# Recurrence's local part in pairs of tiles, its elementwise work on VectorE; the triangular solve and the queries in other places

## Chip, cores and metric

One core of a Trainium2 chip runs the whole program. The time is device microseconds (us) of one execution; of several executions the median is taken. Engines: TensorE (PE, its weight loads PEld), VectorE (DVE), ScalarE (ACT), GpSimd (POOL), SyncE (SP, which here issues most DMAs, in order).

## What is computed

A block of two layers (neighbourhood attention, grouped-query attention, each with a gated side branch) and then a third layer, which the change is about: a norm, eight heads of sparse attention (compressed, selected and window branches, mixed by gates), eight heads of an RWKV-7 recurrence, an output projection with a residual, and a final norm. S is 512 tokens, the width 1024, a head 64 wide. The recurrence, cut to what matters:

```
p = p + shift_mu * (prev - p)                  # prev: the token before
r, k, v, wd, ad = split(p)
decay = exp(-exp(-softplus(-(w0 + tanh(wd) @ w_up)) - 0.5));  a = sigmoid(a0 + ad @ a_up)
kk = normalise(k * k_k);  k = k * (1 + (a - 1) * k_a)
for each token t:   sa = state @ -kk_t
                    state = state * w_t + outer(sa, kk_t * a_t) + outer(v_t, k_t);  y_t = state @ r_t
y = group_norm(y) * gn_w + gn_b + sum(r * k * r_k) * v;   out = x + concat(o_nsa, y * silu(g)) @ w_out
```

## The kernel before

Tokens lie on partitions in four tiles of 128 (TT = 4). A float32 operand of a product is split into a high and a low part: `fetch` casts a weight unit on ScalarE (L147, `whi`) and subtracts on VectorE or GpSimd (L148, `wlo`); `N.lo` says which. The heads of the recurrence go in two halves `hh` of four heads (256 columns). The first two layers hold the tokens in a permuted order; `natural` (L322) copies the activations into the order of time, 16 copies, 8 on VectorE and 8 on ScalarE.

The third layer's part around the change runs so. (1) The last stage of the second layer ends in `middle_norm`, whose rows L710 (`hn`) feed the transposes of all later products. (2) `rwkv_proj_first` (L804) computes r, k and v of half 0, stages them in two activation tiles and stores rows of 768 columns in DRAM (`d_raw`, L812; a second copy holds the shifted mixture). (3) `rwkv_lowrank` (L747) makes decay and `a` of all tokens: one projection, a tanh, eight products `sc` (L769), eight tanh L771 into a ring of two tiles, each stored by ScalarE's queue (`d_low`, L774). (4) r of half 1, then in the next block `rwkv_consts` (L724, which also clears a tile, L733, and writes it over `d_t` in eight DMAs, L736), k and v of half 1, and `natural`. (5) `rwkv_local` (L827), eight times (half, tile): it loads `low` (L837) and the two copies of r, k, v (L841, four buffers `rkv` for both), adds them (L844), normalises k with a Newton rsqrt on 4 columns (L236 to L249), forms cumulated decays on TensorE (`xa`, L865), the transposed factors (L890), the 64-column products `x` (L920), masks them in two instructions per head (L925, L926), applies them to v (L928, L930), and stores six kinds of rows. Six elementwise operations of a tile are GpSimd's: L847, L848, L939, L940, L944, L945. (6) `rwkv_triangles` (L948) loads all 8 x 16 blocks of 32 x 32 (`d_a`, L951); `rwkv_solve` (L957) inverts them with 54 pairs of a multiply (L967) and a subtract (L969) on VectorE, and stores `d_t` (L972). (7) Per tile `rwkv_applied` loads `d_t` (L995) and applies it (L1003) to give K and U (L1015); `rwkv_chain` then walks the state through two chunks of 64 tokens (`VU`, L1042); `rwkv_out` makes the output rows (stored L1105). (8) `nsa_group` (L1297) is the attention of two groups of four heads, 32 blocks of two heads each with a softmax row `n_P` (L1352, L1355, L1359); (9) the output projection (L216, first add L1400) and the final norm end the program.

What sets the order: the program is written in the order above, but between (5) and (8) the generator `products()` (L1581) interleaves the attention's keys, the recurrence's gates (`rwkv_gates`), the queries (`nsa_rows`: L1229 transposes, L1233 `n_qr`) and the scores, and `tail(n)` advances the generator of (7), `steps`, or the outputs, `outs`, at the product numbers of the table `at` (L1599); the numbers from 100 on count blocks of `nsa_group`. Within that a scheduler that simulates a timeline fixes the order of instructions on each engine, and each engine runs its own in order.

```
                next(steps if nxt[1] else outs, None)
                nxt = next(at, None)
```

## Time and profile before

| | |
|---|---|
| median of 3 runs | 1234.04 us (1232.77 to 1237.34) |
| the profiled execution | 1231.49 us, of it the span 1229.7 us |
| busy in the span: PE, PEld, DVE | 1141.6, 1001.5, 847.8 us |
| ACT, POOL | 623.7, 401.8 us |
| instructions | 20522 |
| mean granted TensorE clock | 0.969 of full speed |

The profiled execution is 2.55 us below the median, and 1.8 us of it lie outside the span. Times in the trace count from the start of the span. Busy time of PE holds modelled ends of pipelined matmuls, so that 93% is not 93% of what the engine could do.

### The profile page before, as it was taken

To read this page: it belongs to the slowest core of one execution; us is meant where nothing else is said; L and a number is where in the kernel's file an instruction comes from. 1 tells how busy PE (TensorE), PEld (TensorE's weight loads), DVE (VectorE), ACT (ScalarE), POOL (GpSimd) and SP (SyncE) were. 2 spreads that over 40 slices of the span, in tenths; PEclk is the share of its full clock that TensorE was granted. 3 is DMA by queue.
4 is the path that set the end of the run, shared out by engine and by line. 5 is a ranking of instruction groups with operands and counts; after the bars stand their busy time and mean duration, and the time that the engine had idled before them with its cause. 6 is when DMAs were issued, how large, how long until landed. Compare 5 with 4: busy or idle time off the path is not lost.

```text
span 1229.7 us, 20522 instructions
## 1 busy us (share of the span) xinstructions
PE 1141.6 (93%) x7176; PEld 1001.5 (81%) x7176; DVE 847.8 (69%) x2097; ACT 623.7 (51%) x1355; POOL 401.8 (33%) x553
## 2 busy tenths in 40 slices
...
GB/s 247 116 104 103 104 98 95 99 53 141 88 102 90 82 35 1 69 38 32 52 146 66 149 107 205 239 225 180 192 167 175 162 137 103 241 45 78 189 35 69
DMA packets 87041, 143.26 MB, mean 116 GB/s; under 512 B 21525, under 2 KB 52245, under 8 KB 86938
## 3 DMA queue, kind: packets, MB, share of 16 engines
...
HBM read 114.12 MB, written 27.79 MB: 115 GB/s over the span
## 4 chain that ended last, share of the span: by engine, by line
PE 61%; DVE 18%; DMA 6%; ACT 6%; issue 5%; POOL 3%; SPq 2%; ACTq 0%; DVEq 0%; POOLq 0%
PE mm L205 24%; PE mm L188 5%; PE mm L189 5%; PE mm L190 5%; PE sc L205 3%; PE mm L216 2%; PE u L677 1%; PE tr L492 1%; DVE KT L967 1%; PE tr L670 1%; DVE big L969 1%; PE ch L1003 1%; PE tr L318 1%; DMA rkv<-d_raw 1%; PE u L205 1%
## 5 line engine op out<-in xcount | busy, mean ns | idle before, releaser
L205 PE MATMUL mm<-whi,act 128*128 128x256 f32 (+2 forms) x1344 | 357.4, 324 | 8.7 <-DVE x L347 3.3
L205 PE MATMUL mm<-wlo,act 128*128 128x256 f32 (+2 forms) x896 | 287.5, 321 | 0.4 <-POOL wlo L148 0.4
L205 PEld LDWEIGHTS mm<-whi,act 128*128 128x128 f32 x1344 | 240.9, 195 | 30.2 <-DVE x L347 5.6
L205 PEld LDWEIGHTS mm<-wlo,act 128*128 128x128 f32 x896 | 174.9, 195 | 10.3 <-POOL wlo L148 0.6
L147 ACT CAST whi<-wraw 128x1024 fp32r<-128x1024 f32 (+1 forms) x128 | 133.3, 1043 | 91.5 <-PE mm L205 36.8
L205 PE MATMUL mm<-whi,half 128*128 128x256 f32 (+1 forms) x448 | 145.6, 326 | 3.6 <-DVE half L222 3.6
L148 DVE TENSOR_TENSOR wlo<-wraw,whi 128x1024 fp32r<-128x1024 f32 x87 | 109.7, 1263 | 52.0 <-ACT whi L147 50.0
L148 POOL TENSOR_TENSOR wlo<-wraw,whi 128x1024 fp32r<-128x1024 f32 (+2 forms) x41 | 99.6, 2434 | 132.0 <-DVE rs_y L237 69.9
L188 PE MATMUL mm<-act,whi 128*128 128x512 f32 x312 | 125.4, 402 | 2.7 <-DVE b_qn L547 2.7
L190 PE MATMUL mm<-act,wlo 128*128 128x512 f32 x312 | 124.4, 399 | 0.0
L205 PEld LDWEIGHTS mm<-whi,half 128*128 128x128 f32 x448 | 87.8, 196 | 10.2 <-DVE half L222 4.5
L484 POOL TENSOR_SCALAR a_P<-a_P,a_rd 128x256 f32<-128x256 f32 x64 | 32.9, 517 | 156.6 <-DVE a_rd L483 143.9
L189 PE MATMUL mm<-half,whi 128*128 128x512 f32 x200 | 79.1, 396 | 0.0
L188 PEld LDWEIGHTS mm<-act,whi 128*128 128x128 f32 x312 | 59.6, 191 | 14.4 <-issue 3.6
L190 PEld LDWEIGHTS mm<-act,wlo 128*128 128x128 f32 x312 | 59.5, 191 | 12.0
L663 POOL TENSOR_SCALAR b_P<-b_P,b_rd 128x512 f32<-128x512 f32 x64 | 45.5, 715 | 54.8 <-DVE b_rd L662 44.2
L660 ACT ACTIVATE b_P<-sc,b_mn 128x512 f32<-128x512 f32 x64 | 44.1, 690 | 21.5 <-DVE b_mn L657 13.5
L657 DVE TENSOR_REDUCE b_mn<-sc 128x1 f32<-128x512 f32 x64 | 43.5, 684 | 10.9 <-PE sc L655 10.4
L478 DVE CUSTOM_DVE_ANT_0 a_P<-sc,a_bias 128x256 f32<-128x256 f32 x64 | 26.1, 422 | 34.7 <-PE tr L492 20.1
L222 DVE TENSOR_TENSOR b_pl<-tr,b_ph 128x512 fp32r<-128x512 f32 x64 | 43.3, 683 | 6.0 <-ACT b_ph L221 5.3
L1359 POOL TENSOR_SCALAR n_P<-n_P,b_rd,n_gl 128x128 f32<-128x128 f32 (+3 forms) x64 | 39.0, 616 | 25.5 <-DVE b_rd L1357 6.4
L189 PE MATMUL mm<-act,whi 128*128 128x512 f32 x112 | 45.3, 404 | 0.0
...
## 6 DMA issues: line engine op xcount, KB each, us to landing
...
```

The costliest lines, as they stand in the source:

```text
L147: nc.scalar.copy(hi[:, :m], raw[:, :m])
L148: self.lo.tensor_tensor(lo[:, :m], raw[:, :m], hi[:, :m].bitcast(F32), op=OP.subtract)
L188: nc.tensor.matmul(ps, lhsT=wh[:, kt], rhs=ah[:, kt], start=kt == 0, stop=False)
L189: nc.tensor.matmul(ps, lhsT=wh[:, kt], rhs=al[:, kt], start=False, stop=False)
L190: nc.tensor.matmul(ps, lhsT=wl[:, kt], rhs=ah[:, kt], start=False, stop=kt == KT - 1)
L205: nc.tensor.matmul(ps, lhsT=l, rhs=r, start=i == 0, stop=i == len(ops) - 1)
L222: (eng_lo or nc.vector.tensor_sub)(lo, src, hi.bitcast(F32))
L484: nc.gpsimd.tensor_scalar(w, w, rd, 0.5, op0=OP.mult, op1=OP.mult)
L657: nc.vector.tensor_reduce(mn, ps, axis=AX.X, op=OP.max, negate=True)
L660: nc.scalar.activation(pt, ps, AF.Exp, bias=mn, scale=1.0, accum_out=den)
L663: nc.gpsimd.tensor_scalar(pt, pt, rd, 0.5, op0=OP.mult, op1=OP.mult)
L1359: nc.gpsimd.tensor_scalar(w, w, rd, st["gl"][:, b, gc:gc + 1], op0=OP.mult, op1=OP.mult)
```

## The change

- The eight DMAs that clear `d_t` go into the first layer, from a tile that GpSimd clears.
- r, k and v of half 0 are staged in a ring of four tiles (`pp`) and stored group by group in rows of 256 columns; the two activation tiles are not used for it.
- `natural` stands right behind the projection of half 0; the low-rank part and half 1 use the natural order. The rows of half 1 are then contiguous in DRAM.
- The low-rank part's shift is one VectorE operation instead of three, its ring has three tiles, and its constants are loaded ahead of its projection.
- The local part takes two tiles at a time: inputs of both, one rsqrt on 8 columns, then each tile. The six GpSimd operations of a tile go to VectorE; the scaling of `kr` goes from VectorE (L856) to four ScalarE instructions; the two masks of a head become one of 512 columns. `raw` and `x` get rings of their own (two and three). `d_a` and `d_aq` are stored per pair of heads.
- The solve is a generator: four of its 31 steps after each of the products 8 to 15. The queries (`nsa_rows`) stand ahead of the gates, and the table `at` has other numbers.

```diff
--- before.py
+++ after.py
@@ -724,16 +724,19 @@
     def rwkv_consts(self, pool):
         nc = self.nc
         for name, shape, n in (("tri", [P, 3, P], 384), ("ind", [P, 2], 2)):
-            raw = pool.tile([P, 768], F32, name="rkv", bufs=4)[:, :n]
+            raw = pool.tile([P, 768], F32, name="rkv", bufs=3)[:, :n]
             nc.sync.dma_start(out=raw, in_=self.a[name].rearrange("p a n -> p (a n)") if n > 2 else self.a[name])
             r = pool.tile(shape, F32R, name=name, bufs=1)
             nc.vector.tensor_copy(r.rearrange("p a n -> p (a n)") if n > 2 else r, raw)
             setattr(self, name + "_r", r)
-        zero = pool.tile([P, 768], F32, name="rkv", bufs=4)
-        nc.vector.memset(zero, 0.0)
+
+    def zero_inverses(self, pool):
+        nc = self.nc
+        zero = pool.tile([P, 512], F32, name="zero", bufs=1)
+        nc.gpsimd.memset(zero, 0.0)
         for t in range(TT):
             for h in range(2):
-                nc.sync.dma_start(out=self.head_rows(self.d_t, t, 4 * h, 4), in_=zero[:, :512].rearrange("p (h n) -> p h n", h=4))
+                nc.sync.dma_start(out=self.head_rows(self.d_t, t, 4 * h, 4), in_=zero.rearrange("p (h n) -> p h n", h=4))
...
+        ps = self.cols(("r_wa",), act)
+        d = buf[:, 0]
+        nc.scalar.mul(d, ps, rest)
+        nc.vector.scalar_tensor_tensor(d[:, 1:], ps[:, :S - 1], mu, d[:, 1:], op0=OP.mult, op1=OP.add)
...
-                nc.tensor.matmul(ps, lhsT=l[0:65, t * P:t * P + P], rhs=m[0:65], start=True, stop=True)
-                th = buf[:, 6 + t % 2]
+                nc.tensor.matmul(ps, lhsT=l[:, t * P:t * P + P], rhs=m, start=True, stop=True)
+                th = buf[:, (1, 6, 7)[(4 * j + t) % 3]]
...
-                for t in range(2 * hh):
+                for t in range(2):
                     for d, a in zip(self.d_raw[hh], r):
-                        o = bass.AP(tensor=d.tensor, offset=d.offset + (1 + 16 * (2 * tp + t)) * 768 + 256 * n, ap=[[768, 16], [64 * 768, 8], [1, 256]])
+                        o = (1 + (16, P)[hh] * (2 * tp + t)) * 768 + 256 * n
+                        o = bass.AP(tensor=d.tensor, offset=d.offset + o, ap=[[[768, 16], [64 * 768, 8]], [[768, P]]][hh] + [[1, 256]])
                         nc.sync.dma_start(out=o, in_=a[:, t])
-
-    def rwkv_proj_first(self, act, mu):
-
-        raw = [self.act_tile(self.act, j, F32).rearrange("p k n -> p (k n)") for j in range(2)]
-        full = [a[:, :TT * 768].rearrange("p (t n) -> p t n", t=TT) for a in raw]
-        self.rwkv_proj(act, 0, "rkv", mu, lambda n, tp: [a[:, 2 * tp:2 * tp + 2, 256 * n:256 * n + 256] for a in full])
-        for t in range(TT):
-            for d, a in zip(self.d_raw[0], full):
-                o = bass.AP(tensor=d.tensor, offset=d.offset + (1 + 16 * t) * 768, ap=[[768, 16], [64 * 768, 8], [1, 768]])
-                self.nc.sync.dma_start(out=o, in_=a[:, t])
-        return [a[:, TT * 768:].rearrange("p (a t n) -> p a t n", a=2, t=2) for a in raw]
...
-    def rwkv_local(self, pool, hh, t, par, st):
+    def rwkv_inputs(self, pool, hh, t, par, ss):
 
         nc = self.nc
         tmp = lambda: pool.tile([P, 256], F32, name="rt", bufs=13)
         heads = lambda ap: ap.rearrange("p (h d) -> p h d", d=HD)
         V = nc.vector
-        G = nc.gpsimd
         cs = slice(256 * hh, 256 * hh + 256)
-
         low = pool.tile([P, 2, 256], F32, name="low", bufs=2)
         nc.sync.dma_start(out=low, in_=self.d_low[:, t, :, cs].rearrange("j p n -> p j n"))
-        raw = pool.tile([P, 3, 256], F32, name="rkv", bufs=4)
-        x = pool.tile([P, 3, 256], F32, name="rkv", bufs=4)
+        raw = pool.tile([P, 3, 256], F32, name="rkv0", bufs=2)
+        x = pool.tile([P, 3, 256], F32, name="rkv", bufs=3)
         for o, dst, d in zip((1, 0), (raw, x), self.d_raw[hh]):
             nc.sync.dma_start(out=dst.rearrange("p n m -> p (n m)"), in_=d[o + P * t:o + P * t + P])
-        L, a1 = low[:, 0], low[:, 1]
+        a1 = low[:, 1]
         km, kr = tmp(), tmp()
         V.tensor_tensor(x, x, raw, op=OP.add)
         r, k, v = (x[:, n] for n in range(3))
         nc.sync.dma_start(out=self.d_v[t, :, cs], in_=v)
-        G.tensor_tensor(kr, k, par["k_k"], op=OP.mult)
-        G.tensor_tensor(km, a1, par["k_a"], op=OP.mult)
+        V.tensor_tensor(kr, k, par["k_k"], op=OP.mult)
+        V.tensor_tensor(km, a1, par["k_a"], op=OP.mult)
         V.scalar_tensor_tensor(k, km, 1.0, k, op0=OP.add, op1=OP.mult)
         sq = km
         nc.scalar.activation(sq, kr, AF.Square)
+        V.tensor_reduce(ss, heads(sq), axis=AX.X, op=OP.add)
+        return low, x, kr
+
+    def rwkv_local(self, pool, hh, tp, par, st):
+
         ss = self.small.tile([P, 8], F32, name="l_ss")
-        V.tensor_reduce(ss[:, :4], heads(sq), axis=AX.X, op=OP.add)
-        V.tensor_scalar(ss[:, :4], ss[:, :4], 1e-24, None, op0=OP.max)
-        rs = self.rsqrt(ss[:, :4], 4, "l")
-        V.tensor_tensor(heads(kr), heads(kr), rs[:, :4, None].to_broadcast([P, 4, HD]), op=OP.mult)
+        parts = [self.rwkv_inputs(pool, hh, 2 * tp + j, par, ss[:, 4 * j:4 * j + 4]) for j in range(2)]
+        self.nc.vector.tensor_scalar(ss, ss, 1e-24, None, op0=OP.max)
+        rs = self.rsqrt(ss, 8, "l")
+        for j in range(2):
+            self.rwkv_tile(pool, hh, 2 * tp + j, par, st, parts[j], rs[:, 4 * j:4 * j + 4])
+
+    def rwkv_tile(self, pool, hh, t, par, st, part, rs):
+        nc = self.nc
+        tmp = lambda: pool.tile([P, 256], F32, name="rt", bufs=13)
+        heads = lambda ap: ap.rearrange("p (h d) -> p h d", d=HD)
+        V = nc.vector
+        cs = slice(256 * hh, 256 * hh + 256)
+        low, x, kr = part
+        L, a1 = low[:, 0], low[:, 1]
+        r, k, v = (x[:, n] for n in range(3))
+        for h in range(4):
+            w = slice(64 * h, 64 * h + 64)
+            nc.scalar.mul(kr[:, w], kr[:, w], rs[:, h:h + 1])
         V.scalar_tensor_tensor(a1, a1, 1.0, kr, op0=OP.add, op1=OP.mult)
...
-        ab = pool.tile([P, 4, 2, P], F32, name="abq", bufs=2)
...
+            ab = pool.tile([P, 2, 2, 2, P], F32, name="abq", bufs=2)
...
-                am = pool.tile([P, 256], F32, name="am", bufs=2)
-                V.tensor_tensor(am, ps[:, 0:256], mask, op=OP.mult)
-                V.tensor_tensor(ab[:, h].rearrange("p a n -> p (a n)"), ps[:, 256:512], mask, op=OP.mult)
+                V.tensor_tensor(ab[:, e].rearrange("p j a n -> p j (a n)"), ps.rearrange("p (j n) -> p j n", j=2),
+                                mask[:, None, :].to_broadcast([P, 2, 256]), op=OP.mult)
+                am = ab[:, e, 0].rearrange("p a n -> p (a n)")
...
-        nc.sync.dma_start(out=self.head_rows(self.d_a, t, 4 * hh, 4), in_=ab[:, :, 0])
-        for c in range(2):
-            w = slice(64 * c, 64 * c + 64)
-            nc.sync.dma_start(out=self.d_aq[t, w, 4 * hh:4 * hh + 4], in_=ab[w, :, 1, w])
+            h = 4 * hh + 2 * pr
+            nc.sync.dma_start(out=self.head_rows(self.d_a, t, h, 2), in_=ab[:, :, 1, 0])
+            for c in range(2):
+                w = slice(64 * c, 64 * c + 64)
+                nc.sync.dma_start(out=self.d_aq[t, w, h:h + 2], in_=ab[w, :, 1, 1, w])
         nc.sync.dma_start(out=self.d_y0[t, :, cs], in_=y0.rearrange("p r n -> p (r n)"))
         kg = tmp()
-        G.tensor_tensor(kg, k, e2, op=OP.mult)
-        G.tensor_tensor(e2, b, e2, op=OP.mult)
+        V.tensor_tensor(kg, k, e2, op=OP.mult)
+        V.tensor_tensor(e2, b, e2, op=OP.mult)
         for j, src in enumerate((e2, kg)):
             nc.sync.dma_start(out=self.d_kb[t, j, :, cs], in_=src)
         sq = tmp()
-        G.tensor_tensor(sq, r, k, op=OP.mult)
-        G.tensor_tensor(sq, sq, par["r_k"], op=OP.mult)
+        V.tensor_tensor(sq, r, k, op=OP.mult)
+        V.tensor_tensor(sq, sq, par["r_k"], op=OP.mult)
...
                                         op=OP.mult)
                 nc.vector.tensor_tensor(tv, tv, o, op=OP.subtract)
+            yield
...
+                        if (hf, t) == (1, 0):
+                            N.zero_inverses(pool)
...
-                    rest = N.rwkv_proj_first(act, N.rwkv_mu(pool, 0, 0, 3, "mu0"))
+                    ring = lambda n, tp: [pool.tile([P, 512], F32, name="pp", bufs=4).rearrange("p (t n) -> p t n", t=2) for _ in range(2)]
+                    N.rwkv_proj(act, 0, "rkv", N.rwkv_mu(pool, 0, 0, 3, "mu0"), ring)
+                    act = N.natural(act)
                     N.rwkv_lowrank(pool.tile([P, 8, S], F32, name="low", bufs=1), act)
-                    N.rwkv_proj(act, 1, "r", N.rwkv_mu(pool, 1, 0, 1, "mu1"), lambda n, tp: [a[:, tp] for a in rest])
+                    N.rwkv_proj(act, 1, "r", N.rwkv_mu(pool, 1, 0, 1, "mu1"), ring)
...
-                act = N.natural(act)
...
-                    for t in range(TT):
-                        N.rwkv_local(loc, hh, t, par, st)
+                    for tp in range(2):
+                        N.rwkv_local(loc, hh, tp, par, st)
...
-            N.rwkv_solve(chn, *sv)
+            solve = N.rwkv_solve(chn, *sv)
...
+                for _ in N.nsa_rows(keep, pool, act, st, ns):
+                    yield
                 for _ in N.rwkv_gates(pool, act):
-                    yield
-                for _ in N.nsa_rows(keep, pool, act, st, ns):
                     yield
...
-            at = iter(((10, 1), (14, 1), (14, 0), (14, 1), (21, 0), (21, 1), (100, 0), (100, 1), (102, 0)))
+            at = iter(((17, 1), (18, 1), (18, 0), (19, 1), (20, 0), (20, 1), (100, 0), (100, 1), (102, 0)))
...
             for n, _ in enumerate(products()):
+                for _ in range(4 if 8 <= n < 16 else 0):
+                    next(solve, None)
                 tail(n)
```

**SyncE, ahead of the first tile's loads.** `d_t` are the inverses, `low` and `d_raw` the inputs of the local part, `wraw` weights. Before:

```order
78 L728 DMA rkv<-in_ind 128x2
79 L780 DMA mu<-in_shift_mu 128x2x256
80 L686 DMA k_k<-in_k_k 128x256
81 L736 DMA d_t<-rkv 128x4x128 x8
82 L686 DMA k_a<-in_k_a 128x256
83 L686 DMA r_k<-in_r_k 128x256
84 L837 DMA low<-d_low 128x2x256
85 L802 DMA d_raw_84<-st_8768 16x8x256 x2
86 L802 DMA d_raw_83<-st_8767 16x8x256 x2
87 L841 DMA rkv<-d_raw_81 128x768
```

After:

```order
91 L728 DMA rkv<-in_ind 128x2
92 L789 DMA mu<-in_shift_mu 128x2x256
93 L686 DMA k_k<-in_k_k 128x256
94 L686 DMA k_a<-in_k_a 128x256
95 L686 DMA r_k<-in_r_k 128x256
96 L834 DMA low<-d_low 128x2x256
97 L838 DMA rkv_9028<-d_raw_81 128x768
98 L812 DMA d_raw_84<-st_8820 128x256 x2
99 L838 DMA rkv<-d_raw_82 128x768
```

The eight clears are gone from this place, and the first `rkv` load stands right behind the first `low` load.

**VectorE, the solve.** `big` are the blocks and their inverses, `n_qr` and `st` belong to queries and gates; a wait in brackets names the engine or DMA queue waited for. Before, its start:

```order
1453 L967 TENSOR_TENSOR KT<-big_10239,big_10237 128x31 [waits DMAHW3_49,DVE_49]
1454 L407 SCALAR_TENSOR_TENSOR st_11057<-st_11057,mm 128x512 [waits Activation_49]
1455 L969 TENSOR_TENSOR big_10239<-big_10239,KT 128x31 [waits DVE_49]
1456 L967 TENSOR_TENSOR KT<-big_10239,big_10237 128x60 [waits DMAHW7_49,DVE_49]
1457 L969 TENSOR_TENSOR big_10239<-big_10239,KT 128x2x30 [waits DVE_49]
```

After, a part of its middle:

```order
1484 L984 TENSOR_TENSOR KT<-big_10201,big_10199 128x112 [waits DVE_49]
1485 L407 SCALAR_TENSOR_TENSOR st_11384<-st_11384,mm 128x512 [waits Activation_49]
1486 L984 TENSOR_TENSOR KT<-big_10201,big_10199 128x140 [waits DVE_49]
1487 L986 TENSOR_TENSOR big_10201<-big_10201,KT 128x8x14 [waits DVE_49]
1488 L1251 TENSOR_TENSOR n_qr<-mm,n_qr 64x512 [waits DMAHW7_49,Activation_49]
1489 L986 TENSOR_TENSOR big_10201<-big_10201,KT 128x10x14 [waits DVE_49]
1490 L984 TENSOR_TENSOR KT<-big_10201,big_10199 128x104 [waits DVE_49]
```

Before, seven instructions of gates and queries stand among the solve's 108 (rows 1453 to 1565); after, 19 of queries, scores and gates do (rows 1425 to 1546).

**VectorE, ahead of the first softmax row.** `VU`, `K`, `U` and `state` are the recurrence, `n_pc` the scores, `n_P` the softmax row. Before:

```order
1638 L1015 TENSOR_TENSOR K<-ch,z 128x256 [waits PE_49,Activation_49]
1639 L1015 TENSOR_TENSOR U<-ch,z 128x256
1640 L222 TENSOR_TENSOR n_pcl<-tr,n_pch 128x512 [waits DMAHW1_49,Activation_49]
1641 L1329 COPY n_Vp<-n_Vc 32x128 [waits Pool_49]
1642 L1329 COPY n_Vp<-n_Vc 32x128 x3
1643 L1352 ISA n_P,b_mn<-sc,causal 128x128 [waits DMAHW6_49]
```

After:

```order
1566 L1060 TENSOR_TENSOR VU<-cs,U 64x512 [waits PE_49]
1567 L1347 COPY n_Vp<-n_Vc 32x128 x3
1568 L222 TENSOR_TENSOR n_pcl<-tr,n_pch 128x512 [waits DMAHW2_49,Activation_49]
1569 L1071 TENSOR_TENSOR state_10226<-cs,state_10226 64x4x64 [waits DVE_49,PE_49]
1570 L1071 TENSOR_TENSOR state_10226<-cs,state_10226 64x4x64 [waits DVE_49]
1571 L1064 TENSOR_TENSOR state_10227<-state_10226,GC 64x4x64 [waits DVE_49] x2
1572 L1033 TENSOR_TENSOR K<-ch,z 128x256 [waits PE_49,Activation_49]
1573 L1033 TENSOR_TENSOR U<-ch,z 128x256
1574 L1370 ISA n_P,b_mn<-sc,causal 128x128 [waits DMAHW1_49]
```

Before, 78 rows stand between the solve's last subtract and the first softmax row, four `VU` among them; after, 28, with two `VU`: the second `VU` is the end of the first tile's chain.

## Rows read from the trace of the kernel before

**Rows 1.** Stretches: us; PE, PEld, DVE, ACT, POOL busy (count); clock; DMA share; GB/s

```profile
695.00:711.00 16.00, 13.11 (x84) 11.16 (x83) 15.38 (x50) 11.20 (x20) 0.00 (x0) 1.00 0.57 178
767.00:798.00 31.00, 21.80 (x147) 21.07 (x146) 10.93 (x19) 13.29 (x15) 7.01 (x9) 0.84 0.77 240
798.00:935.00 137.00, 125.69 (x917) 115.82 (x917) 114.20 (x285) 60.30 (x189) 65.72 (x76) 0.87 0.60 186
947.00:985.50 38.50, 29.53 (x212) 27.34 (x211) 37.66 (x115) 8.49 (x12) 20.06 (x22) 0.92 0.60 181
985.50:1071.60 86.10, 78.34 (x590) 71.12 (x588) 38.92 (x83) 24.29 (x40) 25.61 (x39) 0.94 0.54 161
1071.60:1157.60 86.00, 82.11 (x646) 73.41 (x646) 75.94 (x284) 63.35 (x173) 58.54 (x78) 1.00 0.31 105
1157.60:1229.70 72.10, 58.22 (x299) 47.19 (x297) 40.36 (x106) 27.78 (x61) 31.17 (x28) 0.94 0.18 64
```

**Rows 2.** Timeline of ScalarE ahead of the first tile: start, us, instruction, idle before

```profile
771.13 7.63 ACT L330 CAST act<-half 128x512 fp32r<-128x512 f32 x7
778.67 0.58 ACT L771 ACTIVATE low<-sc 128x512 f32<-128x512 f32 x1
...
792.65 0.40 ACT L221 CAST rt_lh<-low 128x256 fp32r<-128x256 f32 x1 [9.77 <-DMA low<-d_low]
```

**Rows 3.** Timeline of SyncE's queue there

```profile
780.54 6.34 SPq L736 DMA_DIRECT2D d_t<-rkv  x8
...
788.65 0.43 SPq L837 DMA_DIRECT2D low<-d_low  x1
```

**Rows 4.** Timelines there, TensorE's first `xa` and VectorE's first add

```profile
793.11 0.58 PE L865 MATMUL xa<-rt_lh,tri 128*128 128x256 f32 x1 [6.81 <-ACT rt_lh L221]
...
798.07 0.96 DVE L844 TENSOR_TENSOR rkv<-rkv 128x768 f32<-128x768 f32 x1 [3.81 <-DMA rkv<-d_raw]
```

**Rows 5.** Waits from 765 to 940: us in total, times, longest

```profile
ACT rt_lh L221 <- DMA low<-d_low: 26.3, 7, 9.8
...
DVE rkv L844 <- DMA rkv<-d_raw: 11.1, 4, 3.8
```

**Rows 6.** VectorE's groups from 798 to 935: count, busy, mean ns, idle before

```profile
L925 DVE TENSOR_TENSOR am<-x,tri 128x256 f32<-128x256 f32 x32 | 13.3, 415 | 2.8 <-PE x L920 2.6
...
L844 DVE TENSOR_TENSOR rkv<-rkv 128x768 f32<-128x768 f32 x8 | 8.7, 1091 | 12.2 <-DMA rkv<-d_raw 11.1 <-DMA wraw<-in_wstream 1.2
L236 DVE TENSOR_SCALAR l_i<-l_ss 128x4 int32<-128x4 int32 x8 | 6.0, 753 | 0.2
...
L894 DVE TENSOR_TENSOR rt<-rt,rkv 128x256 f32<-128x256 f32 x8 | 5.0, 626 | 0.0
...
L856 DVE TENSOR_TENSOR rt<-rt,l_y 128x256 f32<-128x256 f32 x8 | 3.4, 424 | 0.2
```

**Rows 7.** GpSimd's groups in the same stretch

```profile
L148 POOL TENSOR_TENSOR wlo<-wraw,whi 128x1024 fp32r<-128x1024 f32 x6 | 15.1, 2531 | 1.0 <-ACT whi L147 1.0
L848 POOL TENSOR_TENSOR rt<-low,k_a 128x256 f32<-128x256 f32 x8 | 6.8, 845 | 0.0
```

**Rows 8.** Timeline of GpSimd and VectorE from 804.4

```profile
804.52 2.40 POOL L148 TENSOR_TENSOR wlo<-wraw,whi 128x1024 fp32r<-128x1024 f32 x1
...
804.62 2.33 DVE L236 TENSOR_SCALAR l_i<-l_ss 128x4 int32<-128x4 int32 x1
```

**Rows 9.** By line: ns min/median/max, first and last start

```profile
L967 DVE TENSOR_TENSOR KT<-big,big x54: 169/268/2499, 946.7 to 985.0; 128x135 f32<-128x135 f32 x3, 128x80 f32<-128x80 f32 x3, 128x128 f32<-128x128 f32 x3, 128x112 f32<-128x112 f32 x2
...
L1003 PE MATMUL ch<-act,big x64: 272/275/377, 995.2 to 1084.3; 128*128 128x128 f32 x64
...
L1042 DVE TENSOR_TENSOR VU<-cs,U x8: 679/690/695, 1020.7 to 1105.9; 64x512 f32<-64x512 f32 x8
...
L1352 DVE CUSTOM_DVE_ANT_0 n_P<-sc,causal x64: 261/478/685, 1071.6 to 1172.0; 128x128 f32<-128x128 f32 x16, 128x256 f32<-128x256 f32 x16, 128x384 f32<-128x384 f32 x16, 128x512 f32<-128x512 f32 x16
```

**Rows 10.** Timeline of VectorE, one query instruction

```profile
1053.35 0.69 DVE L1233 TENSOR_TENSOR n_qr<-mm,n_qr 64x512 fp32r<-64x512 f32 x1 [4.91 <-ACT n_qr L1232]
```

24 lines of the change are left out of this document (13 added, 11 removed).

## Prediction, on record before the changed kernel ran

> **What bounds the kernel now.** First the busy times by stretch [rows 1]. VectorE is nearly full in three places: the middle norm (15.38 of 16 us), the solve (37.66 of 38.5) and the attention blocks (75.94 of 86, 0.88). In the local part it has 114.20 of 137 us (0.83) and TensorE 125.69, at a clock of 0.87. Two stretches are weak on VectorE: 767 to 798 (10.93 of 31) and 985.5 to 1071.6 (38.92 of 86.1), between the solve and the first softmax row. Where an engine idles there, the question is what it waits for.
>
> From 767 to 798 it is a chain. ScalarE's last tanh of the low-rank part stands behind seven copies of `natural`, 7.63 us [rows 2]. Then SyncE issues eight clears of `d_t` for 6.34 us, and only at 788.65 the first `low` load [rows 3]. ScalarE waits 9.77 us for it [rows 2], TensorE 6.81 us for the cast behind it, and the first add of the local part starts at 798.07 [rows 4]. In the local part the same kinds of wait come back: 26.3 us of ScalarE for `low`, 11.1 us of VectorE for `rkv` [rows 5].
>
> Behind the solve nothing is short of work: the last multiply starts at 985.0, `d_t` is back and applied at 995.2, the first chunk's `VU` comes at 1020.7, and the first softmax row at 1071.6 [rows 9], because 12 of the 16 VectorE rows of the queries, the gates and the chain of half the tiles stand ahead of it. The sum below is therefore one of positions: which work stands ahead of what.
>
> **The change part by part**, against the profiled execution (1231.49, span 1229.7), which lies 2.55 us under the median of the runs.
>
> *Natural copies early.* Eight copies on VectorE now stand among the norm's rows, six ahead of the last `hn`, in a stretch with 0.62 us of idle [rows 1]. At 0.69 us (the other 512-column row, `VU` [rows 9]) six cost 4.1 us. I take +4 (0 to 6).
>
> *Start of the local part.* 7.63 us of copies and 6.34 us of clears leave the chain to the first load, and three VectorE operations of the shift become one. In their place SyncE issues 16 more stores of r, k and v in 256-column pieces. At a clear's 0.79 us each (6.34/8 [rows 3]) that is 12.7 us, most of it while the projections run. Between nothing and 18 I take 12. With the 4 above, the first add comes at 798 + 4 - 12 = 790. The clears' 6.3 us of SyncE and the memset go to the first layer, where the weight loads of the later stages follow on that queue; I cost them at nothing, 6 if a load there is late.
>
> *Local part.* VectorE gets 48 operations of 256 columns. L856, the same kind, takes 0.424 on average, L894 0.626 [rows 6]; I take the first: +20.4 (up to 30). It loses L856 (3.4), 64 masks of 0.415 against 32 of 0.69 (26.6 - 22.1 = 4.5), and half of 88 rsqrt steps. At the stretch's mean of 114.20/285 = 0.40 [rows 1] 44 are 17.6. Seven query rows of 0.69 move in (4.8). Sum: 114.2 + 20.4 - 3.4 - 4.5 - 17.6 + 4.8 = 114, the same load. TensorE gets 143 more matmuls (queries of the first group, and gates) of 125.69/917 = 0.137, 19.6 us: 145 at the old pace. Against that stand the hand-overs to GpSimd that end (each of six per tile took some 0.8 us, L848 [rows 7]), a second tile to work on while one waits, and 0.13 of the clock to win. From 128 (all waits for `low` and `rkv` gone from VectorE's 23 us of idle, and more than half of TensorE's added work covered) to 150 I take 137, no gain in length, while it carries queries that stood behind the solve. ScalarE's 32 scalings are 10 us at its mean of 60.30/189 = 0.32, beside 77 idle. The last mask: about 926. The 12 us to the first solve step (946.7 - 935) stay: 938.
>
> *Solve.* 19 instructions stand among its 108 instead of seven: nine of queries, three of gates, seven of scores, between 0.17 (the shortest solve step [rows 9]) and 0.69 us. Twelve more at 0.45 are 5.4: 38.5 + 5.4 = 44 (42 to 55), the end at 982. What is late next is `d_t`, with TensorE's gates beside it.
>
> *From the solve to the first softmax row.* 86.1 us before. `d_t` comes back in 10 us (985.0 to 995.2), the first `VU` took 25.5 us from there (1020.7), a step of the chain (1105.9 - 1020.7)/7 = 12.2 [rows 9]. In the new order the first softmax row stands behind two `VU` and the second tile's K and U: 10 + 25.5 + 12.2 = 48 at the old pace, with the old fill of queries on TensorE between. Of that fill 68 gate matmuls are left of some 230 instructions, so I take 40 (33 to 50): 1022. That is 46 us off.
>
> *Attention blocks.* What stood ahead of them now runs beside them: six of the eight `VU` instead of four, with their K, U and states, one more output tile and six more softmax rows, some 45 VectorE rows, about 19 us at 0.42. (75.94 + 19)/0.88 = 108; the rows are short and overlap at their ends, so 106 (100 to 114). First final add: 1128.
>
> *Tail.* Six softmax rows with their 21 transposes and 23 products now lie ahead of the first final add: 72.1 - 8 = 64 (60 to 70). End: 1192.
>
> Sum: 1229.7 + 4 - 12 + 0 + 5.4 - 46 + 20 - 8 = 1193; with 1.8 around the span 1195, and 2.55 more against the median: **1198 us** (rounded up).
>
> **A rule against it.** In the row pair at 804.5 a GpSimd cast took 2.40 us and a VectorE operation on four columns, started 0.1 us later, 2.33 [rows 8], against 0.75 for its kind on average [rows 6]. So a GpSimd cast can hold a VectorE instruction to its end. Nine such casts (six of 2.53 [rows 7], three shorter) stay in the local part, and more come with the queries. The Trainium skill, "SBUF — State Buffer", section "Who interferes with whom", says that a VectorE instruction with two SBUF inputs and a GpSimd instruction that reads SBUF shut each other out for the whole instruction. By that rule all 48 moved operations are of the kind that is held; the trace agrees as to the holding, though the held row has one input. By the row of the nearest kind the sum is mine; by the rule it is the second rival.
>
> **Rivals.**
> 1. *The solve is held.* Each of 14 of the 19 instructions among its steps waits for ScalarE, TensorE or GpSimd, and the solve's chain stands behind it on VectorE; the one such row outside waited 4.91 us [rows 10]. At that price the solve takes 44 + 69 us, `d_t`, chain and softmax rows come as much later, and the time is 1267: slower. It decides from (1240 - 1198)/14 = 3 us each. For it: the positions come from a simulated timeline. Against it: the seven rows that stood there before waited for ScalarE too, and VectorE was still busy 37.66 of 38.5 us [rows 1].
> 2. *The local part grows.* The moved operations cost 0.626 or are held by casts (114 + 10 = 124, at the old share of 0.83: 149), and TensorE's queries add the rest: 12 to 20 us longer. 1210 to 1218, still faster. For it: TensorE is at 0.92 there already.
> 3. *The work only changes its place.* The sum of VectorE's work is what it was. If the start gains nothing (the first load stays behind the projections' stores: 40 more DMAs in all, 24 of them in the local part, 32 us at 0.79), the local part grows by 8, and the attention blocks with the chain beside them take 120, the sum of changes is + 4 + 8 + 5.4 - 46 + 34 - 8 = -3: 1231, no change. The Trainium skill, "DMA: Bandwidth & Descriptors", "Rules for kernel authors", wants many small transfers merged into a large one; no row here shows a split transfer.
>
> **Numbers.** My forecast 0.6 (its own range 1184 to 1212), the second rival 0.2, the third 0.1, the first 0.1. Half a per cent, some 6 us, is about what a measurement of this kernel can tell from no change: faster is under 1228, slower over 1240. Faster 0.6 + 0.2 and a little of the third: 0.81; same 0.1; slower 0.09, the first rival. The range for 8 in 10 takes in the second rival and part of the third: 1182 to 1231.
>
> **What would show it.** Right: the first add near 790, no wait of some 10 us for the first `low`; the last mask near 926; the solve in under 55 us with no idle over 3 us among its steps; the first softmax row within 50 us of its end; VectorE at 0.88 or more from there to the first final add, near 1128. The prediction is wrong if the local part takes over 150 us, if the solve ends after 1005, or if the attention blocks take over 115.

## The result: slower, not faster

| | before | after |
|---|---|---|
| median of 17 runs each | 1232.61 us (1225.21 to 1237.34) | 1241.69 us (1232.59 to 1248.73) |
| ratio, 95% interval | | 1.0078 [1.0059, 1.0097] |
| profiled execution, its span | 1231.49, 1229.7 us | 1244.55, 1242.7 us |
| clock of that execution | 0.969 | 0.959 |

The time lies outside the range (1182 to 1231), on the side given 0.09. Busy times of after, from its page; the matmuls are as many as before, 7176:

```profile
PE 1151.7 (93%) x7176; PEld 1009.8 (81%) x7176; DVE 843.3 (68%) x2057; ACT 631.3 (51%) x1387; POOL 370.4 (30%) x512
```

The stretches of after that answer to [rows 1], with the same columns; from the third on: local part, solve, solve to first softmax row, attention blocks, tail.

```profile
695.00:711.00 16.00, 12.47 (x73) 10.30 (x71) 15.65 (x40) 12.65 (x21) 0.00 (x0) 1.00 0.52 164
767.00:788.70 21.70, 21.25 (x156) 18.90 (x155) 9.22 (x14) 8.14 (x12) 5.37 (x9) 1.00 0.80 253
788.70:954.10 165.40, 149.46 (x1049) 137.59 (x1048) 117.37 (x256) 74.73 (x231) 42.47 (x40) 0.87 0.53 167
...
965.60:1010.30 44.70, 35.59 (x218) 31.68 (x218) 40.16 (x127) 12.33 (x18) 17.48 (x22) 0.85 0.55 164
1010.30:1054.30 44.00, 38.03 (x266) 35.60 (x264) 13.91 (x34) 7.96 (x13) 9.92 (x16) 0.84 0.64 186
1054.30:1174.50 120.20, 111.14 (x907) 99.46 (x907) 98.88 (x340) 75.12 (x200) 68.30 (x93) 0.99 0.31 102
1174.50:1242.70 68.20, 52.67 (x252) 40.97 (x250) 33.36 (x81) 21.29 (x44) 26.90 (x20) 0.94 0.19 66
```

The landmarks by line (ns min/median/max, first and last start), as in [rows 9]:

```profile
L841 DVE TENSOR_TENSOR rkv<-rkv,rkv x8: 948/958/2868, 788.7 to 911.5; 128x768 f32<-128x768 f32 x8
...
L984 DVE TENSOR_TENSOR KT<-big,big x54: 158/271/2410, 965.6 to 1010.0; 128x135 f32<-128x135 f32 x3, 128x80 f32<-128x80 f32 x3, 128x128 f32<-128x128 f32 x3, 128x112 f32<-128x112 f32 x2
...
L1060 DVE TENSOR_TENSOR VU<-cs,U x8: 672/688/695, 1041.7 to 1133.7; 64x512 f32<-64x512 f32 x8
...
L1370 DVE CUSTOM_DVE_ANT_0 n_P<-sc,causal x64: 267/482/692, 1054.3 to 1175.1; 128x128 f32<-128x128 f32 x16, 128x256 f32<-128x256 f32 x16, 128x384 f32<-128x384 f32 x16, 128x512 f32<-128x512 f32 x16
```

Two readings. The local part took 165.4 us instead of 136.9, and the attention blocks 120.2 instead of 86.0, while the solve's end stands only 44 us ahead of the first softmax row instead of 86. And TensorE's matmuls went with the time: in the three stretches local, solve to softmax row, blocks, 917, 590 and 646 before [rows 1], 1049, 266 and 907 now. A matmul's share of the blocks' length is what it was: 86.0/646 = 0.133, 120.2/907 = 0.133 us.

### The profile page after: what moved, and what is told of

Its sections match the earlier page's. It is cut to its first block, busy times and chain, and to the rows that moved or that the text cites. A ratio compares the mean times of both kernels' runs of the same rounds, so it can differ in the third digit from the quotient of the medians.

```text
span 1242.7 us, 20552 instructions
## 1 busy us (share of the span) xinstructions
PE 1151.7 (93%) x7176; PEld 1009.8 (81%) x7176; DVE 843.3 (68%) x2057; ACT 631.3 (51%) x1387; POOL 370.4 (30%) x512
## 4 chain that ended last, share of the span: by engine, by line
PE 65%; DVE 18%; DMA 7%; issue 4%; ACT 4%; POOL 2%; ACTq 0%; SPq 0%; DVEq 0%; POOLq 0%
PE mm L205 24%; PE mm L188 5%; PE mm L189 5%; PE mm L190 4%; PE mm L216 3%; PE sc L205 3%; PE u L677 1%; PE tr L670 1%; PE tr L492 1%; PE ch L1021 1%; DMA wraw<-in_wstream 1%; DMA rkv<-d_raw 1%; PE tr L318 1%; PE x L936 1%; DMA big<-d_t 1%
## 5 line engine op out<-in xcount | busy, mean ns | idle before, releaser
L205 PE MATMUL mm<-whi,act 128*128 128x256 f32 (+2 forms) x1440 | 370.1, 324 | 12.1 <-DVE n_qr L1251 4.5
L205 PEld LDWEIGHTS mm<-whi,act 128*128 128x128 f32 x1440 | 254.3, 196 | 35.3 <-issue 6.8
L205 PEld LDWEIGHTS mm<-wlo,act 128*128 128x128 f32 x896 | 175.1, 195 | 10.4 <-issue 0.7
L188 PE MATMUL mm<-act,whi 128*128 128x512 f32 x312 | 126.2, 404 | 3.9 <-DVE b_qn L547 2.7
L205 PE MATMUL mm<-whi,half 128*128 128x256 f32 (+1 forms) x352 | 116.6, 332 | 3.0 <-DVE half L222 3.0
L189 PE MATMUL mm<-half,whi 128*128 128x512 f32 x192 | 76.1, 396 | 0.0
L205 PEld LDWEIGHTS mm<-whi,half 128*128 128x128 f32 x352 | 68.5, 195 | 8.6 <-DVE half L222 3.9
L660 ACT ACTIVATE b_P<-sc,b_mn 128x512 f32<-128x512 f32 x64 | 44.2, 691 | 21.8 <-DVE b_mn L657 13.6
L1377 POOL TENSOR_SCALAR n_P<-n_P,b_rd,n_gl 128x128 f32<-128x128 f32 (+3 forms) x64 | 40.1, 634 | 38.7 <-DVE b_rd L1375 17.2
L478 DVE CUSTOM_DVE_ANT_0 a_P<-sc,a_bias 128x256 f32<-128x256 f32 x64 | 26.1, 422 | 34.7 <-PE tr L492 20.1
L189 PE MATMUL mm<-act,whi 128*128 128x512 f32 x120 | 49.2, 410 | 0.0
```

The source lines that it names most:

```text
L188: nc.tensor.matmul(ps, lhsT=wh[:, kt], rhs=ah[:, kt], start=kt == 0, stop=False)
L189: nc.tensor.matmul(ps, lhsT=wh[:, kt], rhs=al[:, kt], start=False, stop=False)
L205: nc.tensor.matmul(ps, lhsT=l, rhs=r, start=i == 0, stop=i == len(ops) - 1)
L660: nc.scalar.activation(pt, ps, AF.Exp, bias=mn, scale=1.0, accum_out=den)
L1377: nc.gpsimd.tensor_scalar(w, w, rd, st["gl"][:, b, gc:gc + 1], op0=OP.mult, op1=OP.mult)
```

## The experiments

Two questions: what made the local part 28 us longer, and where the 46 us behind the solve went. In the profile of after, the chain of work that ended last (start, us, step) shows the first suspicion: the add of a tile waits for the load of `x`, and that load starts when the tile three back has read its `v` for the last time (L946).

```profile
907.97 0.29 PE x L946 x2
908.28 3.20 DMA rkv<-d_raw
911.64 1.38 issue
```

With three buffers for `x` and two tiles taken together, the second tile of a pair can only be loaded when the first tile of the pair before is done. In the same way the chain stands on 4.32 us of this load at 830.86 and 3.48 at 883.61: 11.0 us in all. That the wait itself is what costs the time is not shown, and the trace of e1 (below) speaks against it: with a fourth buffer its chain stands on three such loads behind the first, 5.14, 5.38 and 4.70 us, longer than in after, and yet its local part is shorter.

### Ring, pairs, and the two halves of the change (e1 to e4)

e1 gives `x` four buffers and `raw` one, in the same memory. e2 keeps the rings and takes one tile at a time.

```diff
-        raw = pool.tile([P, 3, 256], F32, name="rkv0", bufs=2)
-        x = pool.tile([P, 3, 256], F32, name="rkv", bufs=3)
+        raw = pool.tile([P, 3, 256], F32, name="rkv0", bufs=1)
+        x = pool.tile([P, 3, 256], F32, name="rkv", bufs=4)
```

> The changed kernel with its five 768-column buffers divided anew: four for the summed rows x and one for raw, instead of three and two (same memory). Theory R (the ring of three serialises the pairs: the load of x for tile t+3 waits until tile t is done, and a pair needs both of its x before its rsqrt): the local part, first add to last mask, falls from 165 us to 135 to 148, and the end comes 17 to 28 us earlier. Rival L (the local part is long because of the work moved into it: 143 matmuls of queries and gates, 48 VectorE operations that meet GpSimd casts): 160 to 165 us, no change of the end beyond 4 us.

```diff
-        parts = [self.rwkv_inputs(pool, hh, 2 * tp + j, par, ss[:, 4 * j:4 * j + 4]) for j in range(2)]
-        rs = self.rsqrt(ss, 8, "l")
+        part = self.rwkv_inputs(pool, hh, tp, par, ss[:, :4])
+        rs = self.rsqrt(ss[:, :4], 4, "l")
```

> The changed kernel with the local part one tile at a time (rsqrt on 4 columns per tile), the rings, the VectorE operations and all else as changed. Theory R: no pair waits for its second x; with three x in flight the local part falls to 135 to 150 us, end 12 to 25 us earlier. Rival L: the rsqrt chains come back (some 44 short VectorE operations more), 163 to 172 us, end the same or up to 8 us later.

e3 is after with the late part of before (solve in one piece, gates ahead of the queries, the old table `at`); e4 is the reverse, before with the new late part alone.

```diff
-            at = iter(((17, 1), (18, 1), (18, 0), (19, 1), (20, 0), (20, 1), (100, 0), (100, 1), (102, 0)))
+            at = iter(((10, 1), (14, 1), (14, 0), (14, 1), (21, 0), (21, 1), (100, 0), (100, 1), (102, 0)))
```

> The changed kernel with the late part as before: solve in one piece, gates ahead of queries, the old table. Rival L: without the queries the local part falls to 135 to 148 us and the end comes 10 us or more earlier. Theory R: local part 155 to 165 us. Theory C (behind the solve the recurrence's own chain, some 135 us from the first use of the inverses to its last output row, sets the end, whatever stands ahead of the softmax rows): solve 6 us shorter, solve's end to the end of the span within 10 us of the 232 us of the changed kernel, so 1235 to 1247 in all. Rival B (the softmax blocks on VectorE set the end): 244 us or more behind the solve.

> The kernel before with only the late part changed: solve in steps among the products, queries ahead of the gates, the new table. Rival L: the queries lengthen the local part from 137 to 155 us or more, time 1240 to 1255. Theory R: local part 137 to 145 us. Theory C: solve 44 us, and then 228 to 236 us to the end: 1218 to 1235. Rival B, as I forecast it: softmax rows start 40 us behind the solve and the end comes 205 to 212 us behind it: 1195 to 1208.

Measured: e1 1227.9 us, 0.9967 [0.9936, 0.9999] of before; e2 1228.63, 0.9973 [0.9943, 1.0002]; e3 1236.66, 1.0026 [0.9992, 1.0061]; e4 1236.9, 1.0032 [0.9997, 1.0066]. The stretches of e1 (local, solve to softmax row, blocks):

```profile
791.60:927.60 136.00, 123.00 (x914) 113.69 (x913) 108.15 (x250) 65.62 (x217) 31.81 (x29) 0.89 0.61 187
983.70:1064.30 80.60, 72.23 (x544) 67.33 (x544) 33.87 (x79) 21.20 (x34) 18.25 (x24) 0.92 0.53 157
1064.30:1160.40 96.10, 88.55 (x721) 80.59 (x722) 80.94 (x287) 64.18 (x176) 63.19 (x82) 0.98 0.32 105
```

the local part of e2:

```profile
788.30:926.40 138.10, 124.83 (x934) 113.45 (x932) 115.68 (x294) 66.95 (x219) 30.36 (x25) 0.91 0.60 187
```

and of e4 the local part, solve to softmax row, and blocks:

```profile
800.20:932.90 132.70, 119.69 (x912) 108.86 (x911) 114.42 (x285) 59.55 (x189) 63.88 (x71) 0.94 0.61 191
986.30:1065.20 78.90, 70.65 (x544) 66.27 (x544) 33.93 (x77) 21.19 (x34) 18.74 (x26) 0.95 0.55 165
1065.20:1162.00 96.80, 89.96 (x719) 81.72 (x720) 80.92 (x287) 63.99 (x176) 62.99 (x82) 0.96 0.32 104
```

The pairs with the ring of three are what made the local part long, and the kernel slower than before: with a fourth buffer, or without pairs, the part has 136 to 138 us, as before, and the ratio is under 1. But note its matmuls: 914 and 934, not 1049. In the order of after, 135 more matmuls of later products stand in the local part than in e1's; in e1 they stand behind the solve again, and the stretch up to the first softmax row is 80.6 us. The new late part by itself (e4) brought no time at all, and the place itself gained little: its first softmax row stands 78.9 us behind the solve (86.1 before, forecast 40), and the blocks have 719 matmuls and 96.8 us (646 and 86.0 before). It did not lengthen the local part either.

Against what was expected: e1 ended 13.8 us earlier than after by the medians, less than theory R's 17 to 28; e2 13.1, inside its 12 to 25. e3, with a local part of 157.0 us and 235.4 us from the solve's end to the end, is as theories R and C had it. e4 is outside all four of its forecasts.

### What the end waits for, and the moved operations (e5 to e9)

e5 is e1 with the last loop's row of the recurrence read from a tensor that is ready long before, so that the recurrence is left out of its output. If the end waited for the recurrence's chain, the final adds would move up.

```diff
-                nc.sync.dma_start(out=og, in_=N.d_og[t])
+                nc.sync.dma_start(out=og, in_=N.d_y0[t])
```

> As e1_ring, but the last loop reads a DRAM tensor that the local part wrote long before (y0) in place of the recurrence's output rows, so that the output projection no longer waits for the chain; the chain itself still runs. The recurrence's result is left out of the output. Theory C (the chain of the recurrence sets the end): the end comes 10 to 20 us earlier than in e1_ring, 1208 to 1218. Rivals B and P (the softmax blocks, or TensorE's stream of products ahead of them, set it): within 4 us of e1_ring, 1224 to 1232.

e6 is e1 with the six operations of a tile back on GpSimd.

```diff
-        V.tensor_tensor(kr, k, par["k_k"], op=OP.mult)
-        V.tensor_tensor(km, a1, par["k_a"], op=OP.mult)
+        nc.gpsimd.tensor_tensor(kr, k, par["k_k"], op=OP.mult)
+        nc.gpsimd.tensor_tensor(km, a1, par["k_a"], op=OP.mult)
```

> As e1_ring, with the six elementwise operations of a tile back on GpSimd. Theory V (their move saves the hand-overs between VectorE and GpSimd): the local part grows from 136 to 144 to 160 us, end later by as much. Rival L (on VectorE they stand in a full queue and are held by GpSimd casts, so the move is worth nothing): 130 to 138 us, end the same or up to 6 us earlier.

e7 is before with the early part alone (staging, clears, natural copies, low-rank part); the local part and all behind it are those of before.

```diff
-                    rest = N.rwkv_proj_first(act, N.rwkv_mu(pool, 0, 0, 3, "mu0"))
+                    N.rwkv_proj(act, 0, "rkv", N.rwkv_mu(pool, 0, 0, 3, "mu0"), ring)
+                    act = N.natural(act)
```

> The early part of the change alone (clears in the first layer, ring pp, copies of natural behind the first projection, new low-rank part); local part, solve, order of products and table as before. My forecast for it: last norm row 4 to 6 us later, first add 8 to 10 us earlier, end 8 to 10 us earlier, 1219 to 1224. Theory P (TensorE's stream of work from there to the first softmax row is what lasts, 264 to 273 us in all six kernels so far): the first add earlier, the local part longer by about as much, end within 3 us of the kernel before.

e8 is e2 with the rings of e1; e9 is e1, and e12 is e2, with VectorE's natural copies on GpSimd:

```diff
-        engines = iter(TT * (nc.vector.tensor_copy, nc.vector.tensor_copy, nc.scalar.copy, nc.scalar.copy))
+        engines = iter(TT * (nc.gpsimd.tensor_copy, nc.gpsimd.tensor_copy, nc.scalar.copy, nc.scalar.copy))
```

> As e2_single (one tile at a time), with four buffers for x and one for raw. If the ring still holds tiles back there (theory R in full): local part 122 to 132 us, end 5 to 12 us earlier than e2_single, 1216 to 1223. If three in flight are enough for single tiles, or TensorE's load is the limit: 134 to 140 us and 1225 to 1232.

> As e1_ring, with the eight VectorE copies of natural on GpSimd, which is idle in the norm stage (VectorE is full there). If the copies delay the norm's rows: last norm row from 724 back to 717 to 720, the end 3 to 6 us earlier. If the norm is late for another reason, or GpSimd's copies hold VectorE: no change or later.

> As e2_single, with natural's VectorE copies on GpSimd; a candidate that may beat both kernels. By theory P and e9's reason: last norm row 3 to 5 us earlier than in e2_single, the end as much, 1222 to 1226 (0.6 to 0.9 per cent under the kernel before).

Measured: e5 1227.61, 0.9952 [0.9934, 0.9969], the time of e1: the end does not wait for the recurrence's output row, against theory C. e6 1232.15, 0.9992 [0.9966, 1.0018]: the move of 48 operations from GpSimd to VectorE is worth 3 us of the mean, less than either interval is wide, and its local part took 135.3 us, e1's 136.0. e7 1235.21, 1.0028 [1.0003, 1.0054]: its first add came at 789.5 instead of 798.1, and its local part took 144.7 us instead of 136.9:

```profile
789.50:934.20 144.70, 127.31 (x963) 116.17 (x962) 117.97 (x286) 58.98 (x192) 68.87 (x77) 0.93 0.60 180
```

The 8.6 us won at the start are taken back in the next stretch, in which TensorE now does 963 matmuls, 46 more. My own forecast for it, 1219 to 1224, failed. e8 1231.74, 0.9988 [0.997, 1.0006]; e9 1232.44, 0.9994 [0.9966, 1.0023]; e12 1230.47, 0.9982 [0.9957, 1.0006]: none is better than e1. In e9 and e12 the last norm row did come earlier, at 719.8 (723.7 in e1) and 718.2 (720.3 in e2), and the end did not follow; e8's local part took 142.0 us, outside the lengths of both its forecasts.

### Work taken away and put in (e10, e11)

Both on e1. e10 leaves out the two low products of gates and queries, 256 matmuls; e11 writes every mask twice, 32 more VectorE instructions, 21.8 us at 0.68.

```diff
-                ops += [(l1, wh[:, kt]), (l1, wl[:, kt]), (l2, wh[:, kt])]
+                ops += [(l1, wh[:, kt]), (l1, wl[:, kt]), (l2, wh[:, kt])] if low else [(l1, wh[:, kt])]
```

> As e1_ring, but the recurrence's gates and the queries are computed from the high parts alone: 256 of TensorE's matmuls of 256 columns are left out, 30.7 us at the dense spacing of 0.12; their weights are still split. Theory P (from the last norm row on TensorE's own stream sets the end, whatever stands where): 22 to 32 us earlier, 1196 to 1206. Rival C (the chain from the inverses to the last output row, 134 to 140 us in every kernel, sets it): at most 8 us earlier.

```diff
                                 mask[:, None, :].to_broadcast([P, 2, 256]), op=OP.mult)
+                V.tensor_tensor(ab[:, e].rearrange("p j a n -> p j (a n)"), ps.rearrange("p (j n) -> p j n", j=2),
+                                mask[:, None, :].to_broadcast([P, 2, 256]), op=OP.mult)
```

> As e1_ring, with each of the 32 masks written twice: 21.8 us more of VectorE in the local part. Theory P: TensorE has the waits and VectorE the idle time to take most of it, 0 to 8 us later. Rival V (VectorE's load sets the length of the local part): 18 to 24 us later.

Measured: e10 1212.6 us, 0.9838 [0.9783, 0.9893]; e11 1238.33, 1.0032 [1.0, 1.0064]. e10 gained by far the most in the study, and is the only kernel with less work for TensorE: 15.3 us under e1's median (four executions). In the two profiled executions PE's busy time fell by 28.5 us (1143.1 to 1114.6) and the span by 21.7 (1232.9 to 1211.2): 6.8 us went into idle time. Of the busy time, part went into a lower clock, above all in the solve, with 146 matmuls instead of e1's 210 and a clock of 0.70 (e10, then e1):

```profile
936.60:981.50 44.90, 33.46 (x146) 29.18 (x145) 40.80 (x125) 13.38 (x20) 25.00 (x27) 0.70 0.58 169
```

```profile
938.50:983.70 45.20, 35.10 (x210) 31.05 (x208) 43.26 (x117) 13.06 (x19) 22.82 (x31) 0.84 0.59 169
```

The local part of e11, to the last of its masks:

```profile
795.30:959.20 163.90, 149.83 (x1125) 138.04 (x1125) 137.65 (x292) 79.95 (x242) 46.03 (x44) 0.94 0.58 179
```

It grew by 28 us, more than the masks' own 21.8, but the end came only 10 us later than e1's: TensorE did 1125 matmuls in it instead of 914, and had fewer left to do later (157 from the solve to the softmax row, 544 in e1). A stretch that grows or shrinks tells little about the end.

Neither rival came out whole in either run. e10 gained 15.3 us, between rival C's 8 and theory P's 22 to 32; e11 lost 10.4, between theory P's 8 and rival V's 18 to 24. Half or more of the work taken from TensorE reached the end, and about half of what was put on VectorE in the local part: neither engine is the only bound.

### The local part by itself (e13 to e15)

Before with the new local part alone: e14 with after's rings (three for `x`, two for `raw`), e13 with e1's (four and one), e15 with e1's rings and one tile at a time. Of the edit, whose code is in the diff ahead of the prediction, only the loop stands here:

```diff
-                    for t in range(TT):
-                        N.rwkv_local(loc, hh, t, par, st)
+                    for tp in range(2):
+                        N.rwkv_local(loc, hh, tp, par, st)
```

> As e13, with the rings as changed (three and two). Theory R: the pairs are held, the local part takes 12 to 28 us longer than in e13 and TensorE spends more time at the lower clock (mean clock 0.963 or less): 1232 to 1242, 6 to 16 us above e13. Rival (the ring hurts only together with the queries moved into the local part): within 4 us of e13.

> The kernel before with the new local part alone (pairs, VectorE operations, merged masks), four buffers for x and one for raw; early and late parts as before. If the three parts add (by mean time times mean granted clock: early part alone +3 us, late part alone +3, the whole with this ring -4): the local part alone is worth 8 to 10 us, 1222 to 1226 against 1232. If the parts only shift work between stretches of TensorE: within 4 us of the kernel before.

> As e13, one tile at a time. If pairing is worth something by itself: 3 to 8 us above e13. If what helps is the merged masks, the rsqrt being no matter: within 3 us of e13.

Measured: e14 1241.09, 1.0081 [1.0058, 1.0104]; e13 1236.59, 1.0047 [1.0027, 1.0067]; e15 1230.36, 0.9988 [0.9968, 1.0008]. The paired local part alone costs about as much as the whole change. Here, unlike in e1, the fourth buffer mends less than half of it by the ratios; single tiles mend all. The local part, solve to softmax row, and blocks of e14, then the local part of e13 and of e15:

```profile
798.40:950.70 152.30, 141.70 (x1096) 132.57 (x1096) 111.69 (x254) 73.81 (x227) 38.49 (x28) 0.92 0.60 183
1002.80:1043.20 40.40, 34.17 (x214) 29.97 (x213) 20.75 (x44) 11.58 (x20) 12.24 (x25) 0.88 0.72 201
1043.20:1167.60 124.40, 112.26 (x912) 102.15 (x911) 103.20 (x345) 76.33 (x203) 70.33 (x95) 0.95 0.33 105
```

```profile
799.30:943.60 144.30, 132.85 (x994) 123.85 (x992) 111.65 (x252) 69.86 (x223) 29.93 (x24) 0.89 0.60 179
```

```profile
799.30:939.60 140.30, 131.91 (x988) 121.41 (x987) 113.85 (x296) 69.50 (x223) 28.92 (x24) 0.90 0.59 183
```

The main forecasts missed: the local part alone was to gain 8 to 10 us and lost 4.0 (by the medians; within 4 was the rival); the ring was to cost 6 to 16 us and cost 4.5 (3.0 by the means; within 4 was the rival), and 12 to 28 us of the local part, which was 8.0; single tiles were to lose 3 to 8 us or nothing and gained 6. e14 shows one thing more. Solve, queries and table are those of before in it, and yet its first softmax row stands 40.4 us behind the solve. How long that stretch is goes with the matmuls that are left for it (214 here, 266 in after, 544 in e4, 590 before), not with the new order.

### The lower clock

One number more is needed, since the same matmuls ran in all of them but e10. The mean time of a kernel's executions times their mean granted clock is the time that it would have taken at full speed, if each part ran in proportion; the rest, time x (1 - clock), is what the lower level can have cost at most.

| | mean us | mean clock | product | rest |
|---|---|---|---|---|
| before (31 runs beside e1 to e4) | 1232.1 | 0.9691 | 1194.1 | 38.1 |
| after | 1241.5 | 0.9624 | 1194.9 | 46.7 |
| e1 (ring) | 1228.6 | 0.9687 | 1190.1 | 38.5 |
| e2 (single) | 1228.7 | 0.9709 | 1193.0 | 35.8 |
| e4 (new late part) | 1237.2 | 0.9677 | 1197.3 | 40.0 |
| e7 (early part) | 1236.0 | 0.9687 | 1197.3 | 38.7 |
| e10 (256 matmuls less) | 1214.6 | 0.9615 | 1167.8 | 46.8 |
| e14 (local part, pairs) | 1240.5 | 0.9648 | 1196.9 | 43.6 |
| e13 (the same, four buffers) | 1237.5 | 0.9645 | 1193.6 | 43.9 |
| e15 (the same, single) | 1230.2 | 0.9708 | 1194.2 | 36.0 |

Of the 9.4 us between the means of after and before (before's from the executions beside e1 to e4), 8.6 are in the last column; of the 12.9 between after and e1, 8.2. The profiled executions agree in kind: with the same 7176 matmuls PE's busy time is 10.1 us longer in after (1151.7 against 1141.6), its idle time 2.9 (91.0 against 88.1). In after itself, the fastest execution took 1232.59 us at 0.969 and the slowest 1248.73 at 0.957, products of 1194.4 and 1195.0. But the product is a reckoning, no experiment, and a rough one: it scatters by 2.0 us over after's executions, where the times scatter by 3.6, but by 2.5 over e2's, where the times scatter by 1.5 (standard deviations).

Where the profiled execution of after lost it: (1 - clock) x length from first add to first final add, without the short stretch ahead of the solve, is 0.13 x 165.4 + 0.15 x 44.7 + 0.16 x 44.0 + 0.01 x 120.2 = 36.4 us, against 0.13 x 137 + 0.08 x 38.5 + 0.06 x 86.1 = 26.1 by [rows 1]. Less of it was lost from 695 us to the first add (1.7 us, before 5.0), and 3.4 us more ahead of 695, where the change adds only the clears of `d_t` and where this loss varies from 3.4 to 13.7 us over the profiled executions of the study.

In four stretches of 8 us of after's local part (the columns of [rows 1]) the clock is seen to fall:

```profile
848.00:856.00 8.00, 6.66 (x57) 6.16 (x55) 7.01 (x22) 3.32 (x11) 1.75 (x6) 0.94 0.88 259
856.00:864.00 8.00, 8.00 (x45) 7.20 (x45) 4.16 (x12) 2.05 (x5) 1.96 (x1) 0.50 0.34 107
888.00:896.00 8.00, 6.00 (x48) 5.41 (x47) 6.55 (x20) 3.44 (x11) 0.00 (x0) 1.00 0.64 198
896.00:904.00 8.00, 8.00 (x42) 6.41 (x42) 4.65 (x12) 1.36 (x5) 0.00 (x0) 0.50 0.29 96
```

Twice TensorE paused for 1.3 and 2.0 of 8 us while VectorE was busy for 7.0 and 6.6, preparing tiles; in the next 8 us it had work without a gap, and had it at the lower of its two levels (0.50), 45 and 42 matmuls instead of the 57 and 48 of the stretches with the pause.

This does not set the pairs apart. The kernel before, with single tiles, had the same 0.87 in its local part, and the same kind of stretch in it:

```profile
852.00:860.00 8.00, 6.67 (x63) 6.13 (x61) 4.18 (x10) 1.94 (x7) 1.89 (x5) 0.98 0.71 201
860.00:868.00 8.00, 5.42 (x23) 4.96 (x24) 7.77 (x20) 2.86 (x10) 6.42 (x8) 0.50 0.51 166
868.00:876.00 8.00, 8.00 (x45) 7.22 (x46) 5.30 (x20) 4.06 (x12) 0.81 (x2) 0.50 0.42 112
```

The local part of after is longer at the same clock; the clock is lower than before in the solve (0.85 against 0.92) and behind it (0.84 against 0.94).

## Why the prediction was wrong

**The step that failed** is "From the solve to the first softmax row", "That is 46 us off", set against "Attention blocks" (+20) and "Local part" (137, "no gain in length"). Term by term, in the profiled executions:

| change, us | forecast | measured |
|---|---|---|
| start of the local part | -8 | -9.3 |
| local part | 0 | +28.4 |
| from its last mask to the solve | 0 | -0.5 |
| solve | +5.4 | +6.2 |
| solve to softmax row | -46 | -42.1 |
| attention blocks | +20 | +34.2 |
| tail | -8 | -3.9 |
| sum | -37 | +13.0 |

The -46 came nearly true as a number, and by luck. Its mechanism was the place of VectorE's rows; with the new order alone (e4) the stretch lost 7.2 us, and with the old order it could be as short as 40.4 (e14). What made it short in after is that 324 matmuls were no longer in it (590 to 266). TensorE had been busy for 78.34 of its 86.1 us [rows 1], and there was little idle TensorE to put them on elsewhere: 132 went into the local part, 261 into the blocks (69 came from the other stretches). At 0.133 us each the blocks' share alone is 34.7 us, and the blocks grew by 34.2. I had costed what moved there by VectorE's rows (19 us), and the sum has no term for TensorE, which was busy for 82.11 of the 86 us in the blocks. The view that showed it was [rows 1], read for the wrong engine. The Trainium skill, "Perfetto Trace Analysis", "Identifying the Most-Contended Engine", says that matmul busy time is no good measure of how close TensorE is to its roofline, because matmuls are pipelined. The text ahead of the prediction set PE's 93% aside for the same reason; here the count of matmuls in a stretch, times its time per matmul, was the measure that held.

**The local part**, "137": 165.4. The prediction had the matmuls: 143 more, "145 at the old pace", and covered them by hand-overs that end, a second tile to work on, and the clock. 132 more came. At before's 0.149 us per matmul of this stretch they are 19.7 us; the other 8.7 are a slower pace (0.158). So the cover is what failed: e6 shows the hand-overs to be of no weight, the clock did not rise, and the second tile is what e1 and e2 show to cost time with three buffers for `x`. The order by which the pair is loaded was in the diff; my list of what the change adds has no line for a buffer that comes free later. VectorE's load was right, 117.4 us where 114 were forecast, and so did not make the difference. Its wait for `rkv`, which I had taken to go (11.1 us before [rows 5]), is 6.7 us in after and 6.4 in e1, so this wait is not what the fourth buffer took away. This is a bound of 150 passed, as the text said would show it wrong; the blocks' 120.2 pass the bound of 115 as well.

**The clock**, "0.13 of the clock to win" in the local part: nothing was won there (0.87 both times), and 0.07 and 0.10 were lost in the solve and behind it. Both stretches have fewer matmuls to a us: 218 in 44.7 (4.9) instead of 212 in 38.5 (5.5), and 266 in 44.0 (6.0) instead of 590 in 86.1 (6.9). That this is what brings the lower clock is not shown, and the tail of after, with 252 in 68.2 (3.7) at 0.94, does not follow it.

**The rivals.** The third came nearest: the work only changes its place, 120 us for the blocks, as measured, and no change in the sum. By the products above that is the result (1194.9 against 1194.1), and what it missed is in the clock's column, 8.6 us. It told it of VectorE's work, though, and two of its terms were off in opposite ways: the start, which was to gain nothing, gained 9.3 us, and the local part, which was to grow by 8, grew by 28.4. The first, a held solve, did not come: 44.7 us where 44 were forecast, 40.16 of them VectorE's. The second had the right place, at 12 to 20 instead of 28 us. Of its causes the moved operations were not it (e6); the other, TensorE's added matmuls, is the 19.7 us above, though they stand there only with pairs and three buffers (e1, e2).

**Right, and worth nothing.** The first add came at 788.7 (790), with the first wait for `low` at 5.8 us instead of 9.8 [rows 2]:

```profile
785.43 0.41 ACT L221 CAST rt_lh<-low 128x256 fp32r<-128x256 f32 x1 [5.76 <-DMA low<-d_low]
```

The norm's rows with the natural copies among them took 26.0 us instead of 22.8 (+4 forecast), from the first to the start of the last. e7 shows what the earlier start is worth to the end: nothing, 3.6 us lost if anything.

**Open.** Why e4 and e7 need some 3 us more at full clock than before, where e1 needs 4 less. Why a fourth buffer lifts the clock in after (0.9624 to 0.9687) but not where the local part is alone (0.9648 to 0.9645). Why pairs cost 6 us against single tiles in the old surroundings with four buffers (e13 against e15) and nothing in the new ones (e1 against e8). And what brings the clock down: the pauses are read from the profile, stand in the kernel before as well, and no run changed them alone. So the edit that made the change slow is shown, and the way by which it did so only in part: more matmuls in the local part, at a slower pace.
